# A hybrid SSD, conformer and MLP step on one core: three stages whose steps are issued at other points of the matmul stream

## The chip, the cores and the metric

The kernel runs on one core of a Trainium2 chip. The metric is the device time of one execution in microseconds (us), as the median of several runs. Engines are named as in the profile: PE (TensorE, matmuls; PEld are its weight loads), DVE (VectorE), ACT (ScalarE), POOL (GpSimd) and SP (SyncE, which only issues DMAs).

## The reference, cut to what matters

One layer for 512 new tokens and 8 x 4 continued tokens, 544 columns in all, in float32, model width 2048:

```python
h = rmsnorm(x, w)
z, xbc, dt, cf_a, cf_g = split(h @ w_in)
y = ssd_scan(silu(conv4(xbc)), dt, A, h0)          # 4 groups of 8 heads; also new states
y = rmsnorm((y + d_skip * xs) * silu(z), w)
u = silu(layernorm(conv31(cf_a * sigmoid(cf_g))))  # layer norm over 2048 channels
x = x + concat(y, u) @ w_out
h = rmsnorm(x, w)
u = conv3(h @ w_up)                                # 2 * 5504 channels
x = x + (silu(u[:5504]) * u[5504:]) @ w_down
out = rmsnorm(x, w)
```

## The kernel before, in words

**Layout.** Channels lie on the 128 partitions, the 544 columns in two halves of 272. A float32 product is made of three passes: each operand is split into a rounded high part and the rest, and high x high, high x low and low x high are added up in PSUM. For weights the high part is a cast on ACT (L117, later L1249) and the low part a subtraction on POOL or DVE (L118, later DVE, L1258). Activations are split likewise (`Uh`/`Ul`, `Th`/`Tl`, `Ta`).

**Order.** The order of all engines' work is written out by hand: each engine runs its instructions in program order, and semaphores make it wait where data or a buffer is not ready. `run_jobs` goes through jobs; a job is one tile of 128 output channels, made of 4 blocks of 24 matmuls (4 k-tiles, 3 passes, 2 halves). Ahead of each block `pump` loads weights and splits those of the block three further on. Behind each block come one step of `later` (what a finished job left to do), and one `tick`: the functions that `delay` set for it, and one step of the first generator in the queue `bg`. So "one tick later" means one block of matmuls later in PE's order. `at(t, fn)` puts a function on step t of a generator.

**The stages.** (1) The input projection, one job per tile. `ssd_gen(g)` runs behind it for each of the four groups of heads; the last, g = 3, runs beside the jobs z0 to z3, g0 and a0. Its functions are: f0 to f5 per head (f0 a broadcast matmul, L624; f1 `seg` on DVE, L633, and `ecs` on ACT; f3 the masked product `MT` on DVE, L646; f4 the matmuls of a pair of heads, L655 and L659, into one PSUM tile; f5 its evacuation, L665), s12 to s16 and s22 to s24 for the continued tokens, and per sequence q0 (load of the old state `h0`, SP, L741), qy (matmuls that read it, L752), q1 (its decay, POOL, L745), q2 (matmul, L758), q3 (DVE, L761), q4 (store). `wl_on`/`wl_off` give the weights' low parts to DVE for some ticks. Small PSUM tiles come from the pool `paux` (4 buffers), `xdt`, `hst`, `MT`, `XS`, `sb` and `BM` from the right-hand pool `side` (11 buffers), nearly all else from `slots` (76); buffers are handed out again in the order in which they came free. Behind `ssd_gen(3)` in `bg` wait 16 `conv_gen`s, one per conformer tile, 11 steps each.

(2) The first half of the output projection, jobs `oy`. `ln_gen` runs behind it: mean (L1007), then two tiles per tick are centred on DVE (L1019), squared on ACT and added up in `va` (L1027, L1031), then `rsqrt_gen` with its matmul by ones (L238), then `fin(t)` per tile, which makes `Uh[t]` and `Ul[t]` (L1040, L1044).

(3) The second half, jobs `ou`, reads `Uh`/`Ul`. The last of them is job 15; `ou_evac` makes the steps s0 (sum with the residual on DVE, L1162, `xs` on ACT, store) and s1 (Square on ACT, L1168; for job 15 it also spawns the RMS norm's `rsqrt_gen`). `x_pair(k)` makes the operands of k-tiles k and k + 8 of the up-projection out of `xs`, in four steps of ACT casts (L1118) and DVE subtractions (L1119, L1138 to L1145). `Uh`/`Ul` of tiles 0 and 1 lie in a small right-hand pool, `side0`, whose place is taken by the weights' pool `wr` (`up_open`, in the last job); the pool `whl` of the split weights takes the place of `wp`, which held the blocks' weights.

(4) The up-projection by `items`: per pair of tiles 7 products of 24 matmuls (`product`, L1274 to L1276), with `prep_h` (cast, ACT, L1249) and `prep_l` (DVE, L1258) two items ahead; `sum_a` and `sum_b` add weights on DVE (L1236, L1240), and some loads (L1224) have a second DMA from POOL that adds to them (L1226). Then the down-projection and the last norm.

Of the kernel before, what the change touches and what calls it, by code (L numbers as in the profile page):

```python
# [20 lines left out]
NSIDE = 10  # L21
DOWN = [(6, 6), (5, 6), (4, 0)]
U_SPILL = 8
NSTART = 12
STORE_DELAY = 4
EPS = 1e-5
# [3 lines left out]
def hymba_step_kernel(ctx: ExitStack, tc: tile.TileContext, a: dict):  # L30
# [236 lines left out]
    with tc.manual_schedule():  # L267
# [241 lines left out]
        def ssd_gen(g):  # L509
# [4 lines left out]
            ev = {}  # L514
            L = {}

            def at(t, fn):
                ev.setdefault(t, []).append(fn)

            def hw(ap, n):  # L520
                return ap.unsqueeze(2).to_broadcast([n, 8, 64])
# [99 lines left out]
            def head(h):  # L621
                def f0():
                    p = aux()
                    T.matmul(p, lhsT=L["sel"][h // 4][:, h % 4, :], rhs=D["csT"][:, 0:512], start=True, stop=True)  # L624
                    hd[h] = [p]

                def f1():
                    p = hd[h][0]
                    ecs = slot("ecs", [128, 384])
                    S.activation(ecs, p[:, 128:512], AF.Exp)  # L630
                    seg = slot("seg", [128, 512])
                    for c in range(4):
                        V.tensor_scalar(seg[:, c4[c]], p[:, c4[c]], D["cs_tok"][:, c, 8 * g + h:8 * g + h + 1], 0.0, ALU.subtract, ALU.min)  # L633
                    hd[h] = [ecs, seg]

                def f2():
                    ecs, seg = hd[h]
                    S.activation(seg, seg, AF.Exp)
                    Cd = slot("Cd", [128, 384])
                    G.tensor_tensor(Cd, ecs, Ct[:, 128:512], ALU.mult)  # L640
                    hd[h] = [Cd, seg]

                def f3():
                    Cd, seg = hd[h]
                    MT = slot("MT", [128, 512], side=True)
                    V.tensor_tensor(MT, seg, L["CBm"].rearrange("p c i -> p (c i)"), ALU.mult)  # L646
                    hd[h] = [Cd, MT]

                def f4():
                    ops = [(q, *hd.pop(q)) for q in (h - 1, h)]  # L650
                    yps = yp[h // 2] = aux()
                    for c in range(4):
                        for q, Cd, MT in ops:
                            ro = 64 * (q % 2)
                            T.matmul(yps[ro:ro + 64, c4[c]], lhsT=xdt[c][:, q, :], rhs=MT[:, c4[c]], start=True, stop=c == 0)  # L655
                        for q, Cd, MT in ops:
                            ro = 64 * (q % 2)
                            if c:
                                T.matmul(yps[ro:ro + 64, c4[c]], lhsT=hst[c][:, q, :], rhs=Cd[:, (c - 1) * 128:c * 128], start=False, stop=True)  # L659

                def f5():
                    j = h // 2
                    t = 4 * g + j
                    y_t[t] = slot("y")
                    V.scalar_tensor_tensor(pv(y_t[t]), halves(X[j][:, 0:512]), nw[:, DSK, t:t + 1], halves(yp.pop(j)), ALU.mult, ALU.add)  # L665

                if h % 2:
                    at(10 + h, f5)
                    at(9 + h, f4)
                at(7 + h, f3)  # L670
                at(6 + h, f2)
                at(5 + h, f1)
                at(4 + h, f0)
# [64 lines left out]
            def seq(b):  # L738
                def q0():
                    h0[b] = slot("h0", [128, 8, 64])  # L740
                    Y.dma_start(out=f8(h0[b]), in_=a["h0"][g, :, b, :])  # L741

                def q1():
                    hn[b] = h0.pop(b)
                    G.tensor_tensor(hn[b], hn[b], hw(D["etot"][:, b, gs], 128), ALU.mult)  # L745

                def qy():
                    if b == 0:
                        L["ypo"] = aux()
                    h = h0[b]  # L750
                    for j in range(4):
                        T.matmul(L["ypo"][32 * j:32 * j + 32, 0:128], lhsT=L["CM"][:, b, :],  # L752
                                 rhs=h[:, 2 * j:2 * j + 2, :].rearrange("p h x -> p (h x)"),
                                 start=b == 0, stop=b == 7, tile_position=(0, 32 * j))

                def q2():
                    pb[b] = aux()
                    T.matmul(pb[b], lhsT=L["BM"][b // 4][:, b % 4, :], rhs=f8(L["XS"]), start=True, stop=True)  # L758

                def q3():  # L760
                    V.tensor_tensor(hn[b], hn[b], v8(pb.pop(b)), ALU.add)  # L761

                def q4():
                    store(a["o_sssm"][g, :, b, :], f8(hn.pop(b)))

                t = 18 + b // 2
                at(t + 2, q4)
                at(t + 1, q3)
                at(12 + b // 2, q0)
                at(t, q2)  # L770
                at(17, qy)
                at(t - 1, q1)

            def wl_on():
                cur["wl"] = V
# [1 line left out]
            def wl_off():  # L777
                cur["wl"] = None

            at(17, wl_on)  # L780
            for b in range(8):
                seq(b)
            at(21, wl_off)

            def s22():
                L["yo"] = slot("yo", [128, 128])
# [17 lines left out]
                for j in range(4):  # L804
                    V.tensor_tensor(sv(y_t[4 * g + j]), halves(p[:, 128 + 32 * j:160 + 32 * j]), halves(L["yo"][:, 32 * j:32 * j + 32]), ALU.add)

            at(18, s22)
            at(22, s23)
            at(23, s24)
            return program(ev)  # L810


# [188 lines left out]
        def ln_gen():  # L1001
            for _ in range(3):
                yield
            ps = [aux() for _ in range(2)]
            mu = slot("mu")
            for hf in range(2):
                T.matmul(ps[hf][:, 0:NH], lhsT=ones, rhs=ust["acc"][:, hf, :], start=True, stop=True)  # L1007
                V.tensor_scalar(mu[:, hf, :], ps[hf][:, 0:NH], 1.0 / 2048.0, None, ALU.mult)
            for t in range(U_SPILL):
                U_t[t] = slot("U")  # L1010
                Y.dma_start(out=flat(U_t[t]), in_=u_dram[t])
            yield
            order = list(range(U_SPILL, 16)) + list(range(U_SPILL))
            va = slot("va")
            prev = []
            for n in range(0, 16, 2):
                new = []
                for t in order[n:n + 2]:
                    V.tensor_tensor(U_t[t], U_t[t], mu, ALU.subtract)  # L1019
                    sq = slot("sq")  # L1020
                    S.activation(sq, U_t[t], AF.Square)
                    new.append(sq)
                if n == 2:
                    V.tensor_tensor(va, prev[0], prev[1], ALU.add)
                elif n > 2:
                    for q in prev:
                        V.tensor_tensor(va, va, q, ALU.add)  # L1027
                prev = new
                yield
            for q in prev:  # L1030
                V.tensor_tensor(va, va, q, ALU.add)  # L1031
            yield
            yield from rsqrt_gen([va], setr("rs"))

            def fin(t):
                u = U_t.pop(t)

                def f1():
                    Uh[t] = slot("Uh", dt=F32R, side=t < 2)
                    S.copy(Uh[t], u)  # L1040

                def f2():
                    Ul[t] = slot("Ul", dt=F32R, side=t < 2)
                    V.tensor_tensor(Ul[t], u, Uh[t].bitcast(F32), ALU.subtract)  # L1044
                V.tensor_tensor(u, u, R["rs"], ALU.mult)
                S.activation(u, u, AF.Silu, scale=cfw[:, t, 32:33], bias=cfw[:, t, 33:34])
                delay(1, f1)
                delay(2, f2)
            for t in list(range(U_SPILL, 16)) + list(range(2, U_SPILL)) + [0, 1]:
                if t == 0:  # L1050
                    Cur.side = swap("side0", "side1", bufs=4, side="right")
                fin(t)
                yield
            yield
            yield
# [45 lines left out]
        def ou_pre(i):  # L1101
            def f():
                if i == 0:
                    while not idle():
                        tick()
                    load_xr(0)
                if i + 1 < 16:
                    load_xr(i + 1)
                else:
                    delay(0, up_open)  # L1110
                    for k, n in ((5, 0), (6, 1)):
                        for j, f in enumerate(x_pair(k)):
                            delay(n + j // 2, f)
            return f


# [32 lines left out]
        def x_pair(k):  # L1149
            return prep_pair(T_t, k, lambda: xs[k], lambda: xs[k + 8])  # L1150

        NPRE = 5

        def ou_evac(i):
            t = OT[i]
# [385 lines left out]
        x7 = x_pair(7)  # L1541
        prep_h(0)
        prep_l(0)
        drain_later()
        x7[0]()
        prep_h(1)
        fcw = cload("fcw", [128, 86, 4])
# [5 lines left out]
        for q in range(len(items)):  # L1553
            tick()
            if q == 0:
                x7[1]()
                prep_l(1)
                x7[2]()
                sums[-1]()
            prep_h(q + 2)  # L1560
# [124 lines left out]
```

## Time and profile before

| | us |
|---|---|
| median of 3 runs | 2846.84 (2845.62 to 2849.79) |
| the profiled execution, its own time | 2849.48 |
| its span, first to last instruction | 2847.7 |
| PE busy in it | 2798.8 |
| DVE, ACT, POOL busy | 2097.4, 1214.4, 910.8 |

The profile is of one execution. Its times run from the first instruction. A timeline row gives start, duration, engine, line, operation, tiles written and read, shapes, count, and in brackets how long the engine had been idle and what ended that. [...]

### The profile page before, as it was taken

What the parts mean: (1) busy time and instruction counts of PE and PEld (TensorE: products, weight loads), DVE (VectorE), ACT (ScalarE), POOL (GpSimd) and SP (SyncE); (2) the same over time, 40 slices, a digit from 0 to 9 for tenths busy, and PEclk for the clock granted to TensorE, in tenths of its full rate; (3) what the DMA queues carried; (4) which work ended last, traced back from release to release, by engine and by line L of the source; (5) the groups of instructions that cost most, each with busy time, mean ns of one, the idle gap of its engine ahead of it and who ended that gap; (6) DMA issues with size and microseconds to landing.
All of it is one profiled execution on the core that took longest, in us unless ns stands there. A gap on an engine that the chain in (4) does not pass through costs nothing. (4 is left out here: it accounts for less than half of the span.)

```text
span 2847.7 us, 55491 instructions
## 1 busy us (share of the span) xinstructions
PE 2798.8 (98%) x22214; PEld 2758.7 (97%) x22214; DVE 2097.4 (74%) x3192; ACT 1214.4 (43%) x1792; POOL 910.8 (32%) x928
## 2 busy tenths in 40 slices
PE   8999999999999999999999999999999999999997
PEld 7999998999999999999999999999999999999997
DVE  7576565777777778335488888888888887778775
ACT  4545444333333324333344444444444453344344
POOL 4466666766666765511100000000000000100104
PEclk9999999999999999999999999999999999999999
DMA  4233342433332343444467776777777776765761
GB/s 164 81 113 112 97 139 85 130 103 105 106 100 92 97 157 110 134 139 134 147 158 188 193 192 185 195 193 184 196 186 189 196 194 203 174 186 154 172 184 64
DMA packets 194372, 422.30 MB, mean 148 GB/s; under 512 B 38080, under 2 KB 42816, under 8 KB 194112
## 3 DMA queue, kind: packets, MB, share of 16 engines
q1 hardware_dynamic: 177120, 361.07, 40.8%
q0 software_dynamic: 16992, 57.68, 11.5%
q8 instruction: 174, 2.85, 0.4%
q14 instruction: 86, 0.70, 0.1%
HBM read 376.25 MB, written 42.41 MB: 147 GB/s over the span
## 5 line engine op out<-in xcount | busy, mean ns | idle before, releaser
L1276 PE MATMUL st<-Th,sl 128*128 128x272 f32 x2640 | 762.4, 289 | 1.5 <-DVE sl L1258 1.5
L1274 PE MATMUL st<-Th,sh 128*128 128x272 f32 x2640 | 762.5, 289 | 1.5 <-ACT sh L1249 1.5
L1275 PE MATMUL st<-Tl,sh 128*128 128x272 f32 x2640 | 762.0, 289 | 0.0
L118 POOL TENSOR_TENSOR wl<-raw,wh 128x512 fp32r<-128x512 f32 x336 | 450.1, 1342 | 423.8 <-ACT wh L117 364.7
L1249 ACT CAST sh<-wr 128x1024 fp32r<-128x1024 f32 (+3 forms) x343 | 327.1, 954 | 415.9 <-PE st L1275 338.9
L1276 PEld LDWEIGHTS st<-Th,sl 128*128 128x128 f32 x2640 | 496.9, 188 | 2.4 <-DVE sl L1258 2.4
L1274 PEld LDWEIGHTS st<-Th,sh 128*128 128x128 f32 x2640 | 496.9, 188 | 1.7 <-ACT sh L1249 1.7
L1275 PEld LDWEIGHTS st<-Tl,sh 128*128 128x128 f32 x2640 | 497.0, 188 | 0.0
L228 PE MATMUL mm<-xh,wh 128*128 128x272 f32 x2304 | 488.3, 293 | 7.3 <-ACT xh L312 7.3
L228 PE MATMUL mm<-xl,wh 128*128 128x272 f32 x2304 | 480.1, 290 | 4.0 <-DVE xl L314 4.0
L117 ACT CAST wh<-raw 128x512 fp32r<-128x512 f32 x416 | 255.5, 616 | 530.2 <-PE mm L228 419.3
L228 PE MATMUL mm<-xh,wl 128*128 128x272 f32 x2304 | 478.9, 289 | 0.0
L1258 DVE TENSOR_TENSOR sl<-wr,sh 128x1024 fp32r<-128x1024 f32 (+3 forms) x343 | 378.0, 1102 | 55.1 <-ACT sh L1249 55.0
L228 PEld LDWEIGHTS mm<-xh,wh 128*128 128x128 f32 x2304 | 366.0, 189 | 20.4 <-issue 10.6
L228 PEld LDWEIGHTS mm<-xl,wh 128*128 128x128 f32 x2304 | 366.4, 189 | 5.0 <-DVE xl L314 4.9
L228 PEld LDWEIGHTS mm<-xh,wl 128*128 128x128 f32 x2304 | 366.1, 189 | 0.0
L1226 POOL DMA_DIRECT2D wr<-in_w_up x86 | 75.1, 874 | 834.2 <-DVE ws L1240 266.8
L937 DVE SCALAR_TENSOR_TENSOR ax<-w,cfw,ax 128x512 f32<-128x512 f32 x448 | 302.1, 746 | 5.8 <-ACT ax L913 5.8
L1249 ACT CAST sh<-ws 128x1024 fp32r<-128x1024 f32 (+1 forms) x118 | 117.1, 992 | 259.3 <-DVE ws L1236 144.7
L1258 DVE TENSOR_TENSOR sl<-ws,sh 128x1024 fp32r<-128x1024 f32 (+1 forms) x118 | 136.0, 1153 | 31.3 <-ACT sh L1249 22.0
L1226 POOL DMA_DIRECT2D wr<-in_w_down x32 | 27.9, 872 | 366.0 <-DVE pd L1400 143.5
L118 DVE TENSOR_TENSOR wl<-raw,wh 128x512 fp32r<-128x512 f32 x80 | 70.9, 891 | 96.5 <-ACT wh L117 96.5
(318 smaller groups left out, 4999.7 us busy)
## 6 DMA issues: line engine op xcount, KB each, us to landing
wr<-in_w_up SPq DMA_DIRECT2D x215, 512.0 KB, 4.8
raw<-in_w_in SPq DMA_DIRECT2D x292, 256.0 KB, 3.2
wr<-in_w_up POOLq DMA_DIRECT2D x86, 512.0 KB, 8.2
wr<-in_w_down SPq DMA_DIRECT2D x96, 384.0 KB, 3.4
raw<-in_w_out SPq DMA_DIRECT2D x128, 256.0 KB, 2.9
wr<-in_w_down POOLq DMA_DIRECT2D x32, 384.0 KB, 5.7
ad<-ra SPq DMA_DIRECT2D x43, 272.0 KB, 8.7
ar<-ad SPq DMA_DIRECT2D x43, 272.0 KB, 4.0
```

The lines of the kernel that those rows point to most:

```text
L117: S.copy(h[:, :n], r[:, :n])
L118: (cur["wl"] or eng).tensor_tensor(l[:, :n], r[:, :n], h[:, :n].bitcast(F32), ALU.subtract)
L228: T.matmul(o, lhsT=w[:, c], rhs=x[:, hf, :], start=first, stop=last)
L937: V.scalar_tensor_tensor(p, w[:, i:i + 512], wt(i), p, ALU.mult, ALU.add)
L1226: G.dma_start(out=t, in_=more, accum_op=ALU.add)
L1249: S.copy(h, src)
L1258: V.tensor_tensor(l, src, h.bitcast(F32), ALU.subtract)
L1274: T.matmul(outs[0], lhsT=h[:, c], rhs=xh_, start=k == 0, stop=False)
L1275: T.matmul(outs[0], lhsT=h[:, c], rhs=xl_, start=False, stop=False)
L1276: T.matmul(outs[0], lhsT=l[:, c], rhs=xh_, start=False, stop=k == o.K - 1)
```

## The change

Four things are issued at other points. In `ssd_gen(3)` alone f4, f5, q1 to q4, qy, s22 to s24, wl_on and wl_off come one tick later; the program becomes one tick longer. In `ln_gen` the matmul by ones comes three ticks later. `Uh`/`Ul` of four tiles, not two, lie in `side0` (8 buffers, not 4). `x_pair(5)` is made among the steps of the sixth pair of `ou` jobs and no longer in job 15; `x_pair(6)` starts one tick earlier; and of job 15's steps s1 is left until the first item, behind `prep_l(1)`.

```diff
+NS0 = 4
...
-            def at(t, fn):
-                ev.setdefault(t, []).append(fn)
+
+            def at(t, fn, lag=0):
+                ev.setdefault(t + (lag if g == 3 else 0), []).append(fn)
...
-                    at(10 + h, f5)
-                    at(9 + h, f4)
+                    at(10 + h, f5, 1)
+                    at(9 + h, f4, 1)
...
-                at(t + 2, q4)
-                at(t + 1, q3)
+                at(t + 2, q4, 1)
+                at(t + 1, q3, 1)
                 at(12 + b // 2, q0)
-                at(t, q2)
-                at(17, qy)
-                at(t - 1, q1)
+                at(t, q2, 1)
+                at(17, qy, 1)
+                at(t - 1, q1, 1)
...
-            at(17, wl_on)
+            at(17, wl_on, 1)
             for b in range(8):
                 seq(b)
-            at(21, wl_off)
+            at(21, wl_off, 1)
...
-            at(18, s22)
-            at(22, s23)
-            at(23, s24)
+            at(18, s22, 1)
+            at(22, s23, 1)
+            at(23, s24, 1)
...
-            yield
+            for _ in range(4):
+                yield
             yield from rsqrt_gen([va], setr("rs"))
...
-                    Uh[t] = slot("Uh", dt=F32R, side=t < 2)
+                    Uh[t] = slot("Uh", dt=F32R, side=t < NS0)
...
-                    Ul[t] = slot("Ul", dt=F32R, side=t < 2)
+                    Ul[t] = slot("Ul", dt=F32R, side=t < NS0)
...
-            for t in list(range(U_SPILL, 16)) + list(range(2, U_SPILL)) + [0, 1]:
+            for t in list(range(U_SPILL, 16)) + list(range(NS0, U_SPILL)) + list(range(NS0)):
                 if t == 0:
-                    Cur.side = swap("side0", "side1", bufs=4, side="right")
+                    Cur.side = swap("side0", "side1", bufs=2 * NS0, side="right")
...
-                    for k, n in ((5, 0), (6, 1)):
-                        for j, f in enumerate(x_pair(k)):
-                            delay(n + j // 2, f)
+                    for j, f in enumerate(x_pair(6)):
+                        delay(j // 2, f)
...
-        NPRE = 5
+        NPRE = 6
...
-        drain_later()
+        while len(later) > 1:
+            run_later()
         x7[0]()
...
                 x7[1]()
                 prep_l(1)
+                drain_later()
                 x7[2]()
```

## Rows read from the trace of the kernel before

**Rows 1.** The page, part 1: busy time of each engine.
```profile
PE 2798.8 (98%) x22214; PEld 2758.7 (97%) x22214; DVE 2097.4 (74%) x3192; ACT 1214.4 (43%) x1792; POOL 910.8 (32%) x928
```

**Rows 2.** Waits of PE: who waits for whom, us in total, times, longest.
```profile
PE ax L238 <- DVE va L1031: 6.3, 1, 6.3
PE st L1274 <- ACT sh L1249: 4.8, 2, 3.3
...
PE ax L752 <- DMA h<-in_h: 2.0, 2, 1.4
PE ax L655 <- DVE seg L633: 1.8, 1, 1.8
```

**Rows 3.** Stretches: length, busy PE, PEld, DVE, ACT, POOL; clock, DMA share, GB/s.
```profile
520.00:900.00 380.00, 380.00 (x3003) 380.00 (x3002) 285.70 (x437) 137.95 (x206) 255.61 (x280) 1.00 0.33 101
...
1100.45:1107.28 6.83, 5.51 (x20) 5.04 (x21) 4.27 (x4) 1.17 (x2) 3.74 (x3) 0.50 0.39 117
492.88:496.30 3.42, 3.27 (x20) 2.90 (x21) 0.17 (x1) 1.15 (x3) 0.42 (x1) 0.50 0.86 216
...
1421.31:1428.13 6.82, 6.38 (x26) 5.96 (x26) 4.05 (x6) 3.10 (x5) 0.00 (x0) 0.50 0.37 101
```

**Rows 4.** Timeline of PE around the layer norm's matmul by ones.
```profile
1095.07 0.41 PE L228 MATMUL mm<-Yh,wl 128*128 128x272 f32 x2
1101.77 2.18 PE L238 MATMUL ax<-va,ones 128*128 128x272 f32 x4 [6.29 <-DVE va L1031]
```

**Rows 5.** Timeline of DVE and of POOL in the same stretch.
```profile
1098.86 2.86 DVE L1031 TENSOR_TENSOR va<-va,sq 128x544 f32<-128x544 f32 x2
...
1098.12 3.02 POOL L118 TENSOR_TENSOR wl<-raw,wh 128x512 fp32r<-128x512 f32 x2 [2.49 <-ACT wh L117]
```

**Rows 6.** Instructions of L1044, and of the tile Uh: ns, first and last start.
```profile
L1044 DVE TENSOR_TENSOR Ul<-U,Uh x16: 709/1374/1818, 1118.0 to 1164.6; 128x544 fp32r<-128x544 f32 x16
...
L228 PE MATMUL mm<-Uh,wl x512: 284/287/291, 1224.4 to 1417.7; 128*128 128x272 f32 x171
```

**Rows 7.** Timeline of PE in the last SSD group.
```profile
476.26 0.66 PE L655 MATMUL ax<-MT,xdt 128*64 128x128 f32 x8 [1.81 <-DVE seg L633]
...
492.03 0.43 PE L752 MATMUL ax<-h,cb 128*32 128x128 f32 x8 [1.44 <-DMA h<-in_h]
```

**Rows 8.** Timeline of DVE in the last SSD group.
```profile
457.32 1.49 DVE L646 TENSOR_TENSOR MT<-seg,CBm 128x512 f32<-128x512 f32 x1 [0.20 <-PE ax L655]
...
462.79 6.16 DVE L646 TENSOR_TENSOR MT<-seg,CBm 128x512 f32<-128x512 f32 x1
468.87 1.12 DVE L633 TENSOR_SCALAR seg<-ax,tk 128x128 f32<-128x128 f32 x4
```

**Rows 9.** Timeline of PE at the first products of the up-projection.
```profile
1421.29 0.59 PE L1274 MATMUL st<-Ta,sh 128*128 128x272 f32 x1 [3.34 <-ACT sh L1249]
...
1453.09 0.39 PE L1276 MATMUL st<-Ta,sl 128*128 128x272 f32 x1 [0.30 <-DVE sl L1258]
```

**Rows 10.** Timeline of ACT there.
```profile
1420.20 1.04 ACT L1249 CAST sh<-wr 128x1024 fp32r<-128x1024 f32 x1
...
1423.87 0.64 ACT L1168 ACTIVATE sq<-xres 128x544 f32<-128x544 f32 x1
```

**Rows 11.** Timeline of DVE there.
```profile
1421.27 1.23 DVE L1258 TENSOR_TENSOR sl<-wr,sh 128x1024 fp32r<-128x1024 f32 x1 [0.22 <-ACT sh L1249]
1422.41 0.72 DVE L1162 TENSOR_TENSOR xres<-mm,xres 128x544 f32<-128x544 f32 x1
...
1430.39 1.22 DVE L1236 TENSOR_TENSOR ws<-wr,wr 128x1024 f32<-128x1024 f32 x1
```

**Rows 12.** Timelines of SP and of POOL: the first weights of the up-projection.
```profile
1394.96 14.23 SPq L1224 DMA_DIRECT2D wr<-in_w_up  x5
...
1412.22 1.01 POOL L1226 DMA_DIRECT2D wr<-in_w_up  x1 [2.20 <-PE mm L228]
```

**Rows 13.** The page, part 5: the taps of the 31-wide convolution.
```profile
L937 DVE SCALAR_TENSOR_TENSOR ax<-w,cfw,ax 128x512 f32<-128x512 f32 x448 | 302.1, 746 | 5.8 <-ACT ax L913 5.8
```

## The prediction

> **What bounds the kernel now.** I read the busy times first: PE works for 2798.8 of the 2847.7 us [rows 1], so nothing but PE's own order can set the time, and a change that leaves PE's matmuls as they are can gain or lose only what PE waits, and what it runs slowly. Next came the waits of PE by who ended them [rows 2]. Three stages that the change touches hold most of them: the layer norm's matmul by ones (6.3 us, once), the start of the up-projection (4.8 us in two waits for the cast `sh`), and the last SSD group (2.0 us for the old states' DMA, 1.8 us for DVE's `seg`). Elsewhere PE hardly waits: in the 380 us of the convolution stage it is busy throughout [rows 3]. [...] Last came the timelines around each wait, to see what PE would have done instead and who is late next.
>
> What 0.2% is: 5.7 us, about what a measurement of this kernel can tell from no change.
>
> **The layer norm.** PE ends a block at 1095.5 and waits 6.29 us for `va` [rows 4]; the two last additions on DVE run from 1098.86 to 1101.72 [rows 5]. The edit puts three more ticks ahead of the matmul, so three blocks. A block is 24 matmuls; at the pace of the 16 `ou` jobs (1536 matmuls from 1224.4 to 1417.7, [rows 6]) one takes 0.126 us, a block 3.03 us, and three are 9.1 us, and PE comes to the matmul at 1104.6, 2.9 us behind `va`. What is late next is the weights of the second of these blocks: POOL's two `wl` run from 1098.12 to 1101.14 [rows 5], the first of them is that block's and ends near 1099.5, and PE wants it 0.5 us into the block, at 1099.05: a new wait of 0.4 us. Gain: 6.3, and half of the 5.51 us of work at 0.50 [rows 3], 2.75, less 0.4: **8.6 us**. Bounds: 0, if the wait moves whole, and 9.05. What comes later in `ln_gen` (the inverse root, 16 tiles) ends three ticks, 9.1 us, later in PE's order; it ends now with `Ul` at 1164.6 plus 1.8 us, and the first `ou` matmul that reads it starts near 1224 [rows 6], so 58 us of `oy` blocks cover it.
>
> **The last SSD group.** f4 of the third pair of heads waits 1.81 us at 476.26 [rows 7]. The name is `seg`, not `MT`: f4 takes the PSUM buffer that f1 of head 7 reads. One tick later, behind a block of 3.0 us, that read is over. qy waits for the last two old states (2.0 us in all, the longer 1.44 us, [rows 2, 7]), and the clock then stands at 0.50 for 3.27 us of work [rows 3], worth 1.6 us. The loads stay where they are in SP's order, and their place there is set by POOL freeing slots, not by PE; qy comes a block later, less the 1.8 us gained, so 1.4 us later in time, and the wait is gone but for some tenths. Removed: 1.8 + 2.0 + 1.6 = 5.4 us.
>
> What is late next are buffers. With f4 a tick later, the second pair's f4 takes the PSUM buffer of head 6's `p`, and its `seg` runs from 468.87 to 469.99, because the `MT` ahead of it on DVE took 6.16 us [rows 8]. PE now reaches the third pair's f4 at 476.26 - 1.81 = 474.45 [rows 7]; the second pair's new place is a block and s13's few matmuls ahead of that, an estimate of 3.9 us, and has one f4 less in front of it (28 matmuls, eight of them in 0.66 us with their tail, [rows 7]: some 1.6 us), so PE comes there at 468.95. I take a new wait of 1.0 us; 0 if that `MT` is short, as others are, and 7.2 us plus 3.4 us of slow clock if head 6 becomes as late as head 7 now (476.1). [...] Further, `MT` waits already now for an f4 to free its right-hand buffer (0.20 us at 457.32, [rows 8]): the 11 buffers are all in use, so with f4 a tick later DVE stands a block longer ahead of two `MT`, and behind it wait `seg`, z's evacuation and, through ACT, weights. The weights are split three blocks ahead, which covers a block's delay; the cover gone, it costs PE up to the same 3 us. The last `MT` now waits for the landing of the group's state store; its f4 comes two blocks later. The other moved steps (8 POOL decays, 8 matmuls and 8 sums of the old states, 8 stores on SP, the last small products) keep their distance to each other; one block's `wl` goes back to POOL and another to DVE. The convolution generators behind start one tick later, see the rivals. Gain: 5.4 - 1.0 = **4.4 us**, between -5.2 and 5.4.
>
> **The start of the up-projection.** The last `ou` matmul starts at 1417.7 [rows 6] and the first product at 1421.29 [rows 9]. ACT and DVE are the chain: `x_pair(5)` and then `x_pair(6)` alternate between them through job 15, and only then comes the first cast, 1420.20 to 1421.24 [rows 10]. From the first tick of job 15, one block into a job of 96 x 0.126 = 12.1 us that ends at 1418.0, so 1408.9, to 1420.2 the two pairs take 5.6 us each. With pair 5 made earlier (four casts on ACT, eight subtractions on DVE, no DMA, among steps like those of the four pairs ahead of it, where PE does not wait), pair 6 ends 5.6 us earlier, at 1414.6. The cast then meets another bound: its buffer lies in the place of the last block's `wh` (the addresses in the program of before put it there), so it waits for PE to end, near 1418.0, and starts 2.2 us earlier than now. From there DVE is the chain: `sl` 1421.27, the sum with the residual 1422.41 [rows 11], then pair 7, `sl`, the weights' sum at 1430.39 [rows 11]. The Square of 0.64 us at 1423.87 [rows 10] leaves ACT's part of it, worth 0.55 (an estimate: a tenth overlaps the next). So the chain runs 2.7 us ahead. PE still waits in it, three times by my walk through the first ten products, and the half-speed work in it (6.38 us now, [rows 3]) is covered by DVE. At the other end the inverse root comes one item later on DVE; PE waits 0.30 us for `sl` at 1453.09 now [rows 9], so DVE is just in time there, and this costs some 0.3 us. Gain: **2.4 us**; bounds 0, and 5.0 if the cast need not wait for PE's end.
>
> Four tiles in the right-hand pool cost nothing themselves. They move the loads: of five loads on SP the first goes at 1394.96 and the others within the 14.23 us behind it, once job 15 has read tiles 0 and 1 [rows 12]; with four tiles it must have read tile 2 or 3, two k-tiles of 0.76 us more at most, 1.5 us. The adding DMA on POOL, now at 1412.22 [rows 12], moves with them and lands near 1422 (8.1 us as now); its reader is the weights' sum, then at 1427.7. 5 us of cover; gone, each us costs one.
>
> **Sum.** 8.6 + 4.4 + 2.4 = 15.4 us off the profiled execution's 2849.48 us (its span is 2847.7), which gives 2834.1. That execution is 2.6 us above the median of the runs, so on the median the forecast is 2846.84 - 15.4 = **2831.5 us**.
>
> **Rivals.**
> (a) *The SSD part buys a new wait.* For it: both pools are at their limit, and DVE's order is upset by a 6 us `MT` [rows 8]. Against: all this is in time by my walk. Between 0 and -5.2 from this part: 2846.84 - 11.0 = 2835.8 to 2841.0.
> (b) *The layer norm's wait only moves,* since the work in three more blocks delays `va`, or their `wl` come late. For it: DVE and POOL work side by side there [rows 5]. Against: a margin of 2.9 us. 2846.84 - 6.8 = 2840.0.
> (c) *The first cast is free earlier* than I think: 2831.5 - 2.6 = 2829.
> (d) *Slower: the convolutions.* `bg` is a queue, so a program one tick longer starts all 16 convolution generators one block later than their own jobs, and their evacuations and taps fall on other blocks. If in each tile PE once waits for two taps (0.746 us each, [rows 13]), that is 16 x 1.5 = 24 us: 2855. It is slower by over 0.2% from (15.4 + 5.7)/16 = 1.3 us per tile on. For it: DVE is 75% busy there. Against: PE has no wait at all in it [rows 3], and the queue runs some ticks behind its jobs already.
> (e) *The change does not do what it says,* if a later point of issue were undone by buffers: that is (a) and (b) at once, 2844 to 2847.
>
> **How the numbers follow.** The forecast 0.70 (its own range 2828 to 2835), (a) 0.14, (b) 0.05, (c) 0.04, (d) 0.04, (e) 0.03. The range from 2826 to 2841 takes in (a), (b) and (c) and leaves out (d) and (e). Faster by over 0.2% means under 2841.1: the forecast, (c), and most of (a) and (b), 0.91. Within 0.2%: (e), and the upper ends of (a) and (b), 0.05. Slower: (d), 0.04.
>
> **What would show it.** In the profile after: the wait of L238 for `va` gone from PE's list, with at most some tenths at an L228 for `wl`, and no 0.50 stretch there; the wait of L752 gone, L655's gone or about 1 us, then with DVE `seg` as its name and `seg` behind a long `MT`; the first cast starting as the last `ou` matmul ends, and PE idle about 1.2 us before the first product; no new wait in the convolutions. Wrong would be: the first cast ahead of PE's end, `va` later than PE, L655 waiting several us, or waits in 520 to 1060 us.

## The result, and the profile of the changed kernel

The changed kernel takes 2829.92 us in the median of 6 runs (2829.78 to 2831.34), the kernel before 2846.90 (2845.62 to 2849.79) beside it: a ratio of 0.9941, with a 95% interval from 0.9931 to 0.9951. The forecast was 2831.5 with a range from 2826 to 2841. The profiled execution took 2831.34 us, its span is 2829.6, 18.1 us less than the span before.

The page's part 1 of the changed kernel: PE's busy time falls by 7.9 us [rows 1] with the same 22214 matmuls, so some of them ran at a lower clock before (the mean granted clock was 0.993 and is 0.997); the other 10 us are idle time.

```profile
PE 2790.9 (99%) x22214; PEld 2751.4 (97%) x22214; DVE 2093.0 (74%) x3192; ACT 1214.0 (43%) x1792; POOL 911.9 (32%) x928
```

PE's waits in it. The lines have moved by one to three: L239 is L238 of before, L657 is L655, L754 is L752, L1276 and L1278 are L1274 and L1276 (in the runs below the same instruction can stand a few lines further on).

```profile
PE mm L229 <- ACT xh L313: 7.2, 1, 7.2
PE st L1278 <- DVE sl L1260: 5.3, 7, 1.8
PE mm L229 <- DVE xl L315: 5.1, 6, 2.8
PE ax L239 <- DVE acc L347: 2.2, 1, 2.2
PE ax L420 <- DVE dA_tok L415: 1.1, 1, 1.1
PE st L1276 <- ACT sh L1251: 0.9, 1, 0.9
```

Of [rows 2] the wait for `va` (6.3 us), that for the old states (2.0) and that for `seg` (1.8) are gone, and 0.9 us of the 4.8 for `sh` are left. But the waits for `sl` grew. In the kernel before they were

```profile
PE st L1276 <- DVE sl L1258: 2.3, 5, 0.7
```

so the waits for `sh` and `sl` together fall only from 7.1 to 6.2 us; the rest of what the start of the up-projection gains is work that no longer runs at a granted clock of 0.50 (there the products' matmuls of the kernel before start 0.227 us apart, from 1423.17 to 1427.02, and 0.125 us apart at 1.00, from 1428.74 to 1430.99). The clock is not the cause, though: ssd_alone and ln_alone (below) have a single stretch at 0.50 there too (3.4 us, from 1413.60 and 1412.60), start the stage in the old way, and gain 0.3 us in it. The stretches of this kernel (length, busy PE, PEld, DVE, ACT, POOL, then the clock granted to PE, of which 1.00 is the full one, DMA share, GB/s): the convolutions and the layer norm run with PE busy throughout at full clock, and a single stretch at 0.50 is left at the start of the up-projection, where the kernel before had 6.8 us [rows 3] and another 3.4 us from 1434.96.

```profile
520.00:900.00 380.00, 380.00 (x3003) 380.00 (x3002) 288.49 (x439) 133.83 (x200) 257.81 (x282) 1.00 0.33 102
1040.00:1130.00 90.00, 90.00 (x705) 89.57 (x705) 64.57 (x71) 36.52 (x59) 50.44 (x37) 1.00 0.49 151
1380.00:1470.00 90.00, 84.54 (x639) 82.72 (x639) 67.02 (x94) 41.34 (x56) 8.96 (x9) 0.98 0.61 166
1411.13:1414.54 3.41, 3.41 (x18) 3.41 (x17) 2.02 (x3) 1.29 (x2) 0.00 (x0) 0.50 0.00 0
```

**Where the time went, by stage.** PE's matmuls come in the same order in all these kernels, so the n-th matmul of the projections (rows `mm`) and of the products (rows `st`) can be paired between two traces, and the difference of their starts is PE's lead. The table takes it at four places (matmul 2000, at 348 us in the kernel before; 3200, at 547; 8000, at 1167; product matmul 480, at 1492) and gives what each stage between them adds, in us against the profiled kernel before. Nothing is edited ahead of 348 us; what stands in the first column comes with the execution. The runs were made in four groups, each with the kernel before beside it: 2846.90 us for the changed kernel, 2847.36 for the three parts alone and both_early, 2847.09 for heads_only, states_only, ln_one_tick and sl_early, 2848.04 for mt_pool, pairs_back and square_back. Medians of different groups can so differ by some tenths up to 1 us for no reason of the edit, and parts of that size are read from the table.

| kernel | to 348 us | last SSD group | layer norm | up-projection's start | median of the runs |
|---|---|---|---|---|---|
| after | 0.0 | -5.7 | -9.0 | -3.2 | 2829.92 |
| ssd_alone | -1.8 | -5.7 | -2.0 | -0.3 | 2841.41 |
| ln_alone | 0.0 | -1.9 | -8.3 | -0.3 | 2839.36 |
| up_alone | -1.4 | -1.8 | +0.3 | -2.3 | 2844.32 |
| heads_only | -1.7 | -5.9 | -8.4 | -3.2 | 2830.56 |
| states_only | +0.2 | -3.8 | -9.0 | -2.3 | 2833.63 |
| mt_pool | -1.6 | -5.6 | -0.6 | 0.0 | 2843.14 |
| ln_one_tick | -1.1 | -5.7 | -5.1 | -2.4 | 2835.11 |
| pairs_back | 0.0 | -5.7 | -8.9 | -0.9 | 2832.81 |
| square_back | -1.7 | -5.7 | -9.0 | -2.8 | 2830.36 |
| both_early | +0.1 | -5.7 | -9.0 | -4.3 | 2831.27 |
| sl_early | -1.9 | -5.7 | -9.0 | -4.3 | 2828.78 |

(Another 0.1 us between the layer norm and the up-projection is left out.) The forecast had 4.4, 8.6 and 2.4 in the row of the changed kernel.

### The profile page after: what moved, and what is told of

It reads as the page before. It is cut to its first block, busy times and chain, and to the rows that moved or that the text cites. A ratio compares the mean times of both kernels' runs of the same rounds, so it can differ in the third digit from the quotient of the medians.

```text
span 2829.6 us, 55485 instructions
## 1 busy us (share of the span) xinstructions
PE 2790.9 (99%) x22214; PEld 2751.4 (97%) x22214; DVE 2093.0 (74%) x3192; ACT 1214.0 (43%) x1792; POOL 911.9 (32%) x928
## 4 chain that ended last, share of the span: by engine, by line
PE 95%; DVE 2%; DMA 1%; issue 1%; ACT 0%; DVEq 0%; SPq 0%; POOL 0%; ACTq 0%; POOLq 0%
PE mm L229 44%; PE st L1278 13%; PE st L1276 13%; PE st L1277 13%; PE st L229 6%; PE ax L229 2%; DMA x<-in_xT 1%; PE ax L657 1%; PE ax L596 0%; PE ax L626 0%; PE ax L661 0%; DVE sl L1260 0%; DVE o L498 0%; PE ax L754 0%; PE ax L760 0%
## 5 line engine op out<-in xcount | busy, mean ns | idle before, releaser
L1278 PE MATMUL st<-Th,sl 128*128 128x272 f32 x2640 | 762.7, 289 | 4.6 <-DVE sl L1260 4.6
L1276 PE MATMUL st<-Th,sh 128*128 128x272 f32 x2640 | 762.3, 289 | 0.0
L1278 PEld LDWEIGHTS st<-Th,sl 128*128 128x128 f32 x2640 | 496.8, 188 | 5.9 <-DVE sl L1260 5.9
L1276 PEld LDWEIGHTS st<-Th,sh 128*128 128x128 f32 x2640 | 496.9, 188 | 0.2
```

Source lines behind the costliest of these rows:

```text
L1276: T.matmul(outs[0], lhsT=h[:, c], rhs=xh_, start=k == 0, stop=False)
L1278: T.matmul(outs[0], lhsT=l[:, c], rhs=xh_, start=False, stop=k == o.K - 1)
```

## The experiments

### Each part alone: ssd_alone, ln_alone, up_alone

The kernel before with one part of the change each.

> The kernel before with the last SSD group's later steps alone. Theory (three stages, each with its own wait and its own half-speed work): PE's matmuls stand 5.7 us earlier than before behind this stage and stay so to the end, so 2841.2 us; layer norm's wait of 6.3 us and the first cast's wait of 3.3 us are there as before. My forecast of this part was 4.4 us (2842.5). Rival 1 (the stages lean on each other): the 5.7 us shrink or grow by over 1 us in the convolutions, the layer norm or the start of the up-projection. Rival 2 (the program that is one tick longer delays the convolutions): PE waits show up between 520 and 1060 us and the time is 2846.9 or more.

> The kernel before with the layer norm's matmul by ones three ticks later, alone. Theory: the wait of 6.3 us and half of the 5.5 us of work at 0.50 go, 9.0 us, and the matmuls stay 9.0 us earlier to the end: 2837.9 us; no wait for a low part of the weights takes its place (forecast 0.4 us and 8.6 in all: 2838.3). Rival (the wait only moves, the gain seen with all edits came from the earlier SSD stage): 0 to 3 us, 2844 to 2847.

> The kernel before with the edits at the start of the up-projection alone (four right-hand tiles, pair 5 among the sixth pair's steps, pair 6 a tick earlier, the last Square behind the first item). Theory: 3.3 us at the end, 2843.6 us, and only one 0.50 stretch there in place of two; forecast 2.4 us (2844.5). Rival (it only works because the other two parts shifted loads and PE against each other): 1 us or less, 2846 to 2847.

Measured: 2841.41 us (ratio to before 0.9978, 0.9969 to 0.9988), 2839.36 (0.9971, 0.9960 to 0.9981) and 2844.32 (0.9990, 0.9981 to 1.0000), beside 2847.36 for the kernel before. The three medians lie 5.95, 8.00 and 3.04 us below it, 17.0 in all, as much as the whole change. Yet the table shows that this sum is partly chance, and that the parts do lean on each other a little.

*The SSD part reaches into the layer norm*, 2.0 us of it: rival 1 of ssd_alone held there. Counted in rows `mm`, the matmul by ones stands behind 313 blocks in the kernel before, behind 314 here, 316 in ln_alone and 317 in the changed kernel: the program that is one tick longer moves all of `ln_gen` one block against its jobs. PE's wait in ssd_alone and the stretch behind it:

```profile
PE ax L239 <- DVE va L1033: 5.3, 1, 5.3
```

```profile
1096.16:1099.57 3.41, 3.22 (x10) 2.76 (x11) 1.02 (x3) 0.53 (x1) 1.26 (x1) 0.50 0.30 80
```

The wait is 1.0 us shorter, not 3.0, so `va` moves along by most of that block; and the clock stands at 0.50 for 3.4 us and not 6.8 [rows 3]. And the wait of 0.4 us for `wl` that the forecast named, and ln_alone's theory denied, is there in ln_alone, as its timeline of PE shows, while with the extra tick it is not:

```profile
1097.61 0.52 PE L229 MATMUL mm<-Yh,wl 128*128 128x272 f32 x2 [0.53 <-POOL wl L119]
```

*Half-speed work does not follow every wait.* ln_alone and up_alone leave the SSD group as it was and wait there as the kernel before does, but the clock stays at 1.00; the stretch at 0.50 that begins in up_alone's wait of 6.3 us for `va` is 10.2 us long (with 6.07 us of PE's work in it) and not 6.8 (5.51). Stretches of ln_alone, and then of up_alone:

```profile
485.00:500.00 15.00, 13.49 (x159) 12.26 (x156) 10.24 (x15) 5.62 (x9) 11.19 (x10) 1.00 0.62 188
```

```profile
485.00:500.00 15.00, 13.41 (x150) 12.36 (x149) 9.25 (x14) 5.47 (x8) 11.45 (x11) 1.00 0.54 172
1094.42:1104.66 10.24, 6.07 (x23) 5.59 (x24) 7.58 (x7) 2.12 (x4) 6.07 (x4) 0.50 0.27 82
```

That is why both are 1.8 to 1.9 us ahead in a stage that they do not touch: 0.4 to 0.5 us of shorter waits for the old states, and the rest the clock. Of the 5.7 us of the SSD stage only 3.3 to 3.8 are waits that all three of these executions have.

*The up-projection's part* gives 2.3 us alone, near the forecast's 2.4 and not the theory's 3.3, and 3.2 in the changed kernel with the same timeline of ACT and DVE: the 0.50 stretch of the changed kernel (1411.13 to 1414.54) lies ahead of a point where PE would have waited for `sh` anyway, that of up_alone (1428.92 to 1432.34) behind it. Its wait for `sh` is 2.4 us in two, not 0.9 in one.

### The SSD part in halves: heads_only, states_only

The changed kernel with only one of the two groups of steps one tick later.

```diff
 heads_only: only these keep their lag
                     at(10 + h, f5, 1)
                     at(9 + h, f4, 1)
 states_only: these lose it, all others keep it
-                    at(10 + h, f5, 1)
-                    at(9 + h, f4, 1)
+                    at(10 + h, f5)
+                    at(9 + h, f4)
```

> The kernel after, of whose later steps in the last SSD group only f4 and f5 of the heads are kept; the old states' steps and the small products stand where they were. Theory (the old states' loads have their place in time by the buffers that POOL frees, whatever PE does): the 1.8 us wait for seg is gone, but PE comes to qy 1.8 us earlier and waits 3.4 to 3.8 us there in place of 1.5 to 2.0; the edit alone gains nothing, the time is 3.8 us above the kernel after, and up to 1.8 us more where half-speed work follows: 2833.7 to 2835.5. In the layer norm the matmul by ones stands one block earlier, since the program has no extra tick, and the wait of 0.5 us for wl is back. Rival (each moved step removes its own wait): 2.0 us above the kernel after, 2831.9.

> The kernel after, of whose later steps in the last SSD group f4 and f5 of the heads are put back; the old states' steps and the small products stay one tick later. Theory: the wait of 1.8 us for seg at f4 of the third pair is back, and none at qy, which comes a block of 3 us later; 1.8 us above the kernel after, up to 1.7 more with half-speed work: 2831.7 to 2833.4. A masked product MT of about 6 us stands on DVE ahead of it as in the kernel before, if its length comes from where the heads' steps stand; if it is POOL's work that the other steps move, it is as short as in the kernel after. Rival (the later steps of the heads are what matters for both waits, through the buffers): 3.8 us above, 2833.7, with qy waiting too.

heads_only took 2830.56 us (0.9944, 0.9929 to 0.9960), states_only 2833.63 (0.9953, 0.9940 to 0.9967). The first theory fell: with f4 and f5 alone later there is no wait at `qy` either, which starts at 485.35, in its old place in PE's order, and the stage is worth as much as with all steps later. What heads_only loses, 0.6 us, it loses in the layer norm, by the 0.48 us for `wl` that come back with the shorter program. In states_only the theory's mechanism came: 1.9 us lost in the stage, its only wait there the 1.8 us for `seg`, and a long `MT`. Its median lies 0.2 us above the theory's range and at the rival's number, but the rival's wait at `qy` is not there; another 0.9 us is lost at the start of the up-projection, which has its 0.50 stretches in other places. The last two old states are loaded as late as in the kernel before (489.16 us against 488.89), and `qy`, a block later, reads all eight without a wait:

```profile
489.16 0.80 SPq L743 DMA_DIRECT2D h<-in_h  x2
492.31 1.95 PE L754 MATMUL ax<-h,cb 128*32 128x128 f32 x64
```

DVE in it, and POOL beside:

```profile
462.97 6.15 DVE L648 TENSOR_TENSOR MT<-seg,CBm 128x512 f32<-128x512 f32 x1
469.04 1.11 DVE L635 TENSOR_SCALAR seg<-ax,tk 128x128 f32<-128x128 f32 x4
```

```profile
462.83 1.28 POOL L119 TENSOR_TENSOR wl<-raw,wh 128x512 fp32r<-128x512 f32 x1
464.07 1.35 POOL L863 TENSOR_TENSOR sq<-sq,sq 128x544 f32<-128x544 f32 x1
465.39 0.99 POOL L642 TENSOR_TENSOR Cd<-ecs,Ct 128x384 f32<-128x384 f32 x1
466.34 1.26 POOL L119 TENSOR_TENSOR wl<-raw,wh 128x512 fp32r<-128x512 f32 x1
467.57 1.00 POOL L642 TENSOR_TENSOR Cd<-ecs,Ct 128x384 f32<-128x384 f32 x1
```

POOL's five instructions follow each other without a gap and at their usual length (`wl` 1.28 and 1.26 us, `sq` 1.35, `Cd` 0.99 and 1.00; the medians in the kernel before are 1.29, 1.37 and 1.01); DVE's `MT` ends at 469.12, 0.55 us behind the last of them (468.57). In the changed kernel the same `MT` starts while POOL's `sq` runs:

```profile
460.98 0.77 DVE L648 TENSOR_TENSOR MT<-seg,CBm 128x512 f32<-128x512 f32 x1 [3.83 <-PE ax L657]
463.98 1.84 DVE L648 TENSOR_TENSOR MT<-seg,CBm 128x512 f32<-128x512 f32 x1
465.74 1.11 DVE L635 TENSOR_SCALAR seg<-ax,tk 128x128 f32<-128x128 f32 x4
470.20 0.69 DVE L648 TENSOR_TENSOR MT<-seg,CBm 128x512 f32<-128x512 f32 x1 [2.06 <-PE ax L657]
470.81 1.12 DVE L635 TENSOR_SCALAR seg<-ax,tk 128x128 f32<-128x128 f32 x4
```

```profile
463.44 1.83 POOL L863 TENSOR_TENSOR sq<-sq,sq 128x544 f32<-128x544 f32 x1
465.23 1.47 POOL L642 TENSOR_TENSOR Cd<-ecs,Ct 128x384 f32<-128x384 f32 x1
```

`MT` ends at 465.82, again 0.55 us behind a POOL instruction (465.27), but behind the first one; here POOL's `sq` and `Cd` are the longer ones, 1.83 and 1.47 us in place of 1.35 and 0.99. The idle times of 3.83 and 2.06 us in front of two `MT` are DVE standing a block longer ahead of f4, as forecast. They shift DVE against POOL; that this shift is what makes `MT` short is read from these rows, and no run tests it by itself.

### One instruction on another engine: mt_pool

The kernel before, no step moved:

```diff
-                    V.tensor_tensor(MT, seg, ...)
+                    (G if g == 3 and h == 4 else V).tensor_tensor(MT, seg, ...)
```

> The kernel before, in which one instruction changes its engine: the masked product MT of head 4 in the last SSD group, which took 6.16 us on DVE from 462.79 until just behind the end of POOL's unbroken run of five instructions (468.40), is made by POOL itself. No step is moved. Theory, formed after the heads' later steps alone removed both waits of this stage: that one held instruction makes seg of heads 6 and 7, POOL's work behind it and with it the freeing of buffers for the last old states late by some 6 us, and both waits come from it. Without it the 1.8 us for seg and the 1.5 to 2.0 us for the old states' loads are gone or under 0.5 us together, and the time falls by 3.3 to 3.8 us, up to 5.7 with the half-speed work: 2841.4 to 2843.8. Rival 1 (the places of the steps against the buffers set the waits, the held instruction is a symptom): both waits stay, 2846 to 2848. Rival 2 (POOL's longer run delays wl instead): a new wait of PE at L228 for wl of 1 us or more.

2843.14 us (0.9983, 0.9974 to 0.9993), 4.9 us below the 2848.04 of the kernel before beside it. Both waits are gone, no new one for `wl` has come, and the stage is worth 5.6 us, nearly the 5.7 of the change's whole SSD part. DVE and POOL in it:

```profile
464.67 3.93 DVE L646 TENSOR_TENSOR MT<-seg,CBm 128x512 f32<-128x512 f32 x1 [0.27 <-PE ax L655]
468.85 1.13 DVE L633 TENSOR_SCALAR seg<-ax,tk 128x128 f32<-128x128 f32 x4 [0.25 <-ACT ecs L630]
```

```profile
463.61 1.27 POOL L646 TENSOR_TENSOR MT<-seg,CBm 128x512 f32<-128x512 f32 x1
464.84 0.99 POOL L640 TENSOR_TENSOR Cd<-ecs,Ct 128x384 f32<-128x384 f32 x1
465.80 1.28 POOL L118 TENSOR_TENSOR wl<-raw,wh 128x512 fp32r<-128x512 f32 x1
467.04 1.01 POOL L640 TENSOR_TENSOR Cd<-ecs,Ct 128x384 f32<-128x384 f32 x1
```

POOL needs 1.27 us for it. Now the next `MT` is the long one, 3.93 us until 468.60, 0.55 us behind the end of POOL's run (468.05), but `seg` of head 7 starts at 468.85 and no longer at 474.99 (1.6 us of this is the first column of the table), in time for f4. So the one long instruction caused both waits, and the rivals fell. The path can be followed in the rows, the kernel before first and then mt_pool. Behind `MT` on DVE stands z's evacuation, for which ACT idles ahead of a table load; behind that ACT makes the `ecs` for which `seg` of head 7 waits. And the last two old states are loaded earlier; in the kernel before SP had waited 8.4 us for POOL's `z`.

```profile
470.69 1.28 ACT L845 ACT_TABLE_LOAD   x1 [8.09 <-DVE z L844]
488.89 0.80 SPq L741 DMA_DIRECT2D h<-in_h  x2
```

```profile
464.48 1.28 ACT L845 ACT_TABLE_LOAD   x1 [2.37 <-DVE z L844]
483.39 0.80 SPq L741 DMA_DIRECT2D h<-in_h  x2
```

Why `MT` ends behind one POOL instruction in one order and behind four or five in another, no run shows.

### Fewer ticks in the layer norm: ln_one_tick

```diff
-            for _ in range(4):
+            for _ in range(2):
```

> The kernel after with the layer norm's matmul by ones one tick later than in the kernel before, not three. Theory (va's end does not depend on where PE's matmul stands): in the kernel after va ends at 1098.1 and the matmul starts at 1101.9; two blocks of 3.03 us earlier PE comes at 1095.9 and waits 2.2 us, and half-speed work behind it costs 0 to 2.8 us: 2832.1 to 2834.9. Rival (the added blocks push va back, so that part of the wait moves along): more than 3 us of wait, or va ahead by as much as PE and no wait.

2835.11 us (0.9959, 0.9945 to 0.9973), 0.2 us above the range; PE waits as worked out:

```profile
1097.00 1.20 PE L239 MATMUL ax<-va,ones 128*128 128x272 f32 x4 [2.28 <-DVE va L1033]
```

So `va` does not depend on where this matmul stands. The stage loses 3.9 us, 2.3 of wait and 1.6 behind it, where the clock stands at 0.50 from 1098.04 to 1101.45; another 0.8 us is lost at the up-projection's start, which holds 0.50 stretches in other places than the changed kernel.

### The start of the up-projection undone in parts: pairs_back, square_back

```diff
 pairs_back
-                    for j, f in enumerate(x_pair(6)):
-                        delay(j // 2, f)
+                    for k, n in ((5, 0), (6, 1)):
+                        for j, f in enumerate(x_pair(k)):
+                            delay(n + j // 2, f)
-        NPRE = 6
+        NPRE = 5
 square_back
-        while len(later) > 1:
-            run_later()
+        drain_later()
...
-                drain_later()
```

> The kernel after with pair 5 made in job 15 ahead of pair 6, as before; the four right-hand tiles and the later Square stay. Forecast's term: pair 6 ends 5.6 us later, at 1405.6 in place of 1400.0, so the first cast starts at 1405.6 and not at PE's end (1403.03): 2.2 to 2.6 us later, and so are the products from the tenth on: 2832.1 to 2832.5. With the run that puts the Square back, this splits the term of this stage. Rival (the four tiles and the moved loads are what makes the start earlier): under 1 us, 2830 to 2831.

> The kernel after with job 15's last step, the Square, in its old place in the chain behind the last job. Forecast's term: 0.55 us in the chain, less 0.3 us that it costs later, so the products from the tenth on are 0.25 to 0.6 us later than in the kernel after: 2830.2 to 2830.5. Rival (the engine that does it has slack there, since the other engine's subtractions set the pace): no difference in the chain, and the 0.3 us is gained: 2829.6.

2832.81 us (0.9951, 0.9936 to 0.9966; 0.3 above the range) and 2830.36 (0.9942, 0.9927 to 0.9957). In the table the pairs are worth 2.4 us and the Square 0.5. ACT's first cast in pairs_back comes straight behind pair 6, and PE idles 3.27 us ahead of product 0 in place of 0.93:

```profile
1404.84 0.64 ACT L1121 CAST Th<-tr 128x544 fp32r<-128x544 f32 x1 [1.55 <-DVE tr L1148]
1405.39 1.04 ACT L1252 CAST sh<-wr 128x1024 fp32r<-128x1024 f32 x1
```

### The buffers of the first cast: both_early, sl_early

In the changed kernel ACT's first cast waits 3.05 us for PE's last block, whose end is at 1403.0:

```profile
1399.34 0.65 ACT L1120 CAST Th<-tr 128x544 fp32r<-128x544 f32 x1 [1.55 <-DVE tr L1147]
1403.03 1.04 ACT L1251 CAST sh<-wr 128x1024 fp32r<-128x1024 f32 x1 [3.05 <-PE mm L229]
```

Two kernels lay out the split weights' buffers otherwise; the order of all instructions stays. both_early takes the buffers of `sl` ahead of those of `sh`:

```diff
+        l0 = [whl.tile(..., tag="l", bufs=3, ...) for _ in range(3)]
+        l0[0], l0[1] = l0[1], l0[0]
...
-            l = whl.tile(..., tag="l", bufs=3, ...)
+            l = l0.pop(0) if l0 else whl.tile(..., tag="l", bufs=3, ...)
```

sl_early puts one of the three buffers of `sl` ahead of those of `sh`, and two behind:

```diff
+        l2 = [whl.tile(..., tag="l2", bufs=1, ...)]
...
-            l = whl.tile(..., tag="l", bufs=3, ...)
+            if q % 3 == 2:
+                l = l2.pop() if l2 else whl.tile(..., tag="l2", bufs=1, ...)
+            else:
+                l = whl.tile(..., tag="l", bufs=2, ...)
```

> The kernel after, with the split weights' two groups of buffers laid out the other way round, so that the first cast sh and its low part sl lie over buffers of the last stage that are free one block before its end, and not over those that its last block reads. Theory (the first cast waits for the end of PE's last block, 3.0 us at 1403.03, through its buffer alone): the cast starts at 1400.0 as its engine comes free, sl ends near 1402.3, product 0 follows the last block with no gap, the sum with the residual starts at 1403.1 in place of 1405.25, and all behind is 2.2 us earlier: 2827.7 us. Rival 1 (the first cast waits for PE or for the weights' loads by another way): no change, 2829.9. Rival 2 (the chain behind is set by the loads with the adding DMA or by the cast of the second item): product 0 gains 1.1 us and less than 0.5 us is left at the tenth product, 2829.4 or more.

> The kernel after with the buffers of the split weights laid out so that both the first cast sh and the first low part sl lie over buffers that are free a block before the last stage's end (in the run before this only sh did: it started at 1400.30, but sl still waited until 1403.06, and the chain behind gained 1.0 us). Theory (only these two buffers hold the chain back): sl ends near 1402.6, the sum with the residual starts as PE's last block ends, product 0 has no wait, the chain of the vector engine is 2.1 us ahead of the kernel after, and so is PE from the tenth product on: 2827.8 us. Rival (something else is late next, the adding DMA's landing at 1406.7 or the cast of the weights' sum): product 0 gains 1.1 us, and at the tenth product no more than the 1.0 us of the run before is left, 2828.9.

both_early: 2831.27 us (0.9942, 0.9927 to 0.9957). The cast went ahead to 1400.30 as its buffer allows, but `sl` did not; its own buffer still lay over one that PE's last block reads:

```profile
1403.14 1.23 DVE L1260 TENSOR_TENSOR sl<-wr,sh 128x1024 fp32r<-128x1024 f32 x1 [2.31 <-PE mm L229]
1404.29 0.71 DVE L1164 TENSOR_TENSOR xres<-mm,xres 128x544 f32<-128x544 f32 x1
```

So half of the chain's expected 2.2 us came, 1.1 in the table. The medians do not show it: both_early's is 1.4 us above that of the changed kernel. Its profiled execution (2830.55 us) is 0.8 us below the changed kernel's (2831.34), and the two begin alike. sl_early: 2828.78 us (0.9936, 0.9924 to 0.9949). Both are early, the sum with the residual starts as PE ends, and product 0 (1401.17) follows the last block (1400.92) without a gap:

```profile
1399.20 1.23 DVE L1264 TENSOR_TENSOR sl<-wr,sh 128x1024 fp32r<-128x1024 f32 x1 [0.33 <-ACT sh L1251]
1401.37 0.72 DVE L1164 TENSOR_TENSOR xres<-mm,xres 128x544 f32<-128x544 f32 x1 [0.94 <-PE mm L229]
```

Against the changed kernel PE is 1.1 us ahead at product 0, 2.2 at product 1, but 0.5 at product 3 and 1.0 from product 10 on. Between them lies the stretch at 0.50:

```profile
1412.60:1416.01 3.41, 3.41 (x16) 3.41 (x17) 2.70 (x6) 1.59 (x2) 0.00 (x0) 0.50 0.46 160
```

The theory held for the first two products and the rival's number for the end. sl_early is the best of these kernels, 1.0 us better than the changed one by the trace and 1.1 by the medians; their intervals overlap, so the runs alone do not part them.

## Why the prediction was right, point by point

**What bounds the kernel** was read rightly: PE's order alone set the time, and all that was gained is PE's waits and half-speed work. The sum was somewhat small: in the profiled executions the three terms come to 17.9 us, not 15.4, and in the medians to 17.0.

**The layer norm**, forecast 8.6 us, came to 9.0. The mechanism is shown by ln_alone (8.3) and by ln_one_tick, whose smaller step leaves 2.3 us of the wait. The 0.4 us for `wl` are real (0.53 in ln_alone, 0.48 in heads_only) but not in the whole change. The step that missed it is "The edit puts three more ticks ahead of the matmul": it is four blocks, since the SSD program's extra tick moves `ln_gen` too. That block moves `va` as well: by itself it takes 1.0 us off the wait (ssd_alone), and in the changed kernel the matmul stands 3.8 us behind `va` (1101.9 against 1098.1), where the forecast had 2.9. The text had that extra tick only as a danger for the convolutions.

**The last SSD group**, forecast 4.4 us, came to 5.7. Removed were the waits of 1.8 and 2.0 us, as said, and 1.9 more, where the forecast had 1.6 for the work at 0.50; the other 0.3 us is not explained. Of the two causes given, "qy comes a block later" is enough by itself: states_only does that beside the long `MT` and the late loads, and `qy` does not wait. It is not the only one, for heads_only removes `qy`'s wait without moving `qy`, and mt_pool removes both without moving any step. "One tick later, behind a block of 3.0 us, that read is over" stays open: no run has the later f4 beside a long `MT`, and in the changed kernel `seg` of head 7 starts at 470.81 and not at 474.99. What the forecast did not see is where the old waits came from: the 6.16 us `MT` was taken for an obstacle to the new order, and it was their cause. The mis-sized term is the new wait of 1.0 us, which did not come, because `MT` took 1.84 us. That `MT` would be as long in the new order was my estimate from its 6.16 us in the old one, and it failed. In all four cases read here it ends 0.55 us behind the end of a POOL instruction: in the changed kernel (1.84 us) behind the first, in mt_pool (3.93) behind the fourth, in the kernel before (6.16) and states_only (6.15) behind the fifth. That fits a wait for POOL's work; what sets its length, no run shows.

**The half-speed work** was added, at half of its length, in the layer norm and the SSD group, as the profiled execution had it. No run shows the half: with a matmul every 0.227 us at 0.50 and every 0.125 at 1.00, 0.45 of such work goes, 2.5 us of the 5.51 and 1.5 of the 3.27 (estimates from these numbers). Nor does such work follow every wait: behind the 1.8 us for `seg` the kernel before has no stretch at 0.50. ln_alone and up_alone show that the same SSD waits come without it. For a median this term of the SSD group is between nothing and that 1.5 us.

**The start of the up-projection**, forecast 2.4 us, came to 3.2; in up_alone, states_only and ln_one_tick it is 2.3 to 2.4. The pieces were right: pairs 2.4 by pairs_back (2.2 forecast), the Square with its later price 0.5 (0.25 forecast), the first cast at PE's end (1403.03). What the sum left out is where the half-speed stretch falls: even ssd_alone and ln_alone, which start this stage as the kernel before does, have 0.3 us less in it.

**Rivals.** (a) did not come: no wait of f4 or qy is left. (b) is refuted by ln_alone. (c) is refuted for this change, and both_early shows what held the cast, its buffer; free of it the stage gains 1.1 us and not the 2.6 of the rival. (d) PE is busy for 380.00 of 380.00 us from 520 on, and for 160.00 of 160.00 from 900 to 1060, with the generators one block later. (e) is refuted by the waits that went.

## What to carry to other kernels

When an engine waits, look for the instruction upstream that took many times its usual length before moving steps: here one product that took 6.16 us beside POOL's work, where the median of its line is 0.78, made two waits, and one change of engine removed both. A generator that gets a step more moves all that is queued behind it, so count blocks at the later waits too. And where a stage change re-uses memory, the first casts of the new stage can wait for whatever lies under their buffers, as here by 3.05 us; the order in which buffers are laid out is worth reading.

## What had not been expected of the hardware

The product `MT` on DVE, 0.78 us in the median of the 32 in the kernel before, took 6.15 us beside five POOL instructions in an unbroken run that kept their usual length (0.99 to 1.35 us), 3.93 beside four and 1.84 where it ended behind the first, each time 0.55 us behind the end of a POOL instruction. And the same waits of PE did not bring the same time at a granted clock of 0.50: those of the SSD group 3.4 us in one execution and none in two others, the 6.3 us for `va` 6.8 us in one and 10.2 in another. By the table that moves the gain of one edit by 0.3 to 1.4 us.
